# A decoder layer on one core: first weights and x as contiguous blocks, pooling differences issued sooner, centres before scales

## The chip, the cores and the metric

The kernel runs on one core of one Trainium2 chip. The metric is the device time of one execution in microseconds. The kernel before took 388.74 us (median of three runs, 388.48 to 389.14).

## What is computed

One layer of a decoder for 256 tokens of width 1024, in float32. The input x is projected once (w_in): 512 columns u for a pooling mixer and 512 each of q, k and v for attention with 8 heads of 64. With 256 tokens and blocks of 256 there is one block, so that the attention is plain causal softmax. The pooling mixer takes trailing-window means minus the token, for four windows of 128 channels each, then a linear map for each group:

```python
for g, w in enumerate((2, 4, 8, 16)):
    groups.append((c_hi - c_lo) / count - uf[..., sl])     # sums over the last w tokens
mixed = jnp.einsum('bsgc,gcd->bsgd', pooled, w_pool)
mix = concat([mixed * pool_scale, attention], -1) @ w_out
h = layer_norm(2**0.25 * x + mix, ln1_g, ln1_b)
h = layer_norm(2**0.25 * h + cross_attention(h, mem, w_xq, w_xkv, w_xo), ln2_g, ln2_b)
h = layer_norm(2**0.25 * h + (silu(h @ w_gate) * (h @ w_up)) @ w_down, ln3_g, ln3_b)
```

The cross-attention has 4 heads of 256 over 256 memory tokens; the feed-forward width is 2816.

## The kernel before, in words

**Products.** Each float32 operand is split into a high part of type float32r (a cast on ScalarE, `nc.scalar.copy`, L92 for weights and L300 for activations) and a low part, the rest (a subtraction on VectorE, L93 and L301). A product is three matmuls that add up in a PSUM bank: high x high, high x low, low x high (`three`, L234, and the like in `proj_t` and `product_qk`).

**The stream of weights.** `Stream` (L42) holds all weight tiles w0 to w124 in the order of their use. `fetch` issues the DMA of a tile into a raw buffer (seven of them; the first seven tiles have homes of their own), nearly always on the SyncE queue (SP). `prepare` makes the high and the low part of the next tiles and then fetches further ones; a raw buffer is free again when VectorE has made the low part. `get` hands out a tile and prepares up to eight tiles ahead. The order of the instructions on each engine is the order in which the Python program issues them; nothing is reordered, so that what stands behind a waiting instruction on its engine waits too.

**The start (L358 to L381).** `keep_busy(9)` fills TensorE with matmuls of zeros (`spark`, made by a VectorE memset) while the first data come. Then x^T arrives in pieces `xr` (tile rows 0, 1, 2-3, 4-5, 6-7) and the weights of q and k, columns 512 to 1535 of w_in, in tile rows of 128 x 1024, the first three in two halves of 512 columns each (w0 to w5). w0 goes through the queue of ScalarE, all others through SP. `product_qk(k)` (L341) multiplies tile row k into four banks: for each half of 512 columns the matmuls with the high part of the weights, each column block with xTh and then xTl, then those with the low part. Then follow v (w11 to w14), u (w15 to w18) and the keys of the memory, `xk` (w19 to w26).

In DRAM, w_in is an array of 1024 rows of 8 KB, and x_t one of 128 rows of 8 KB. A transfer of w0 reads 128 pieces of 2 KB, 8 KB apart; one of x's first tile rows 128 pieces of 1 KB, 8 KB apart; v's tiles have 2 pieces of 2 KB for each partition.

**Attention and pooling, interleaved by hand (L502 to L541).** `run(gen, n)` advances a projection by n steps, each of three matmuls for xk and u. Between the steps stand the pieces of attention (`scores`, `probs_t`, `attend`) and of the pooling: when half of u is done, ScalarE copies it to `upad` (L490) and GpSimd adds up the windows (`windows`, L457); VectorE subtracts (`pool_diff`, L467: upad = win / w - upad, in place), TensorE multiplies by w_pool (`mix_pool`, bank `pm`, L473), ScalarE and VectorE split the result. `probs_t` (banks `pt`, L433 to L435) transposes probabilities, and VectorE copies them to `sb` (L438). Banks of this kind rotate through four PSUM buffers.

**Norms (`Norm`, L548).** `sum` adds residual and product (L562), `measure` takes statistics (L565), `stats` joins them (L570, L572) and lets GpSimd raise the variance to the power -0.5 (L573, `rs`). `centre` is (r - mean) * g (L578, needs no `rs`), `scale` is r * rs + b (L584). `finish` (L587) does centre and scale for the first 512 columns, then for the others. Behind the second norm, `transpose_tok` (bank `tp`, L311) turns the result for the next product: the transposes of the first 128 tokens are placed between the last steps of the xo projection (L730 to L735), those of the second 128 between steps of the first gate product `gu0` (L757 to L762).

**The tail (L782 to L824).** The down projection of the second 128 tokens ends in pieces of 512, 256 and 256 columns. The sums of the first 512, of the next 256 and of the last 256 columns stay in their PSUM banks (`in_bank`, L806, and L820), and `finish` (L786) centres and scales them in the order centre 0-511, centre 512-767, scale 0-511, store, scale 512-767, store (on ScalarE's queue), centre 768-1023, scale 768-1023, store.

Of the kernel before, what the change touches and what calls it, by code (L numbers as in the profile page):

```python
# [8 lines left out]
F32 = mybir.dt.float32  # L9
# [5 lines left out]
P = 128  # L15
D = 1024
S = 256
T = S // P
KD = D // P
# [18 lines left out]
def r32(t):  # L38
    return t.bitcast(F32)


class Stream:  # L42


    def __init__(self, nc, pool):
        self.nc, self.pool = nc, pool
        self.src, self.raws, self.tiles, self.homes = [], [], [], []
        self.loads, self.splits = {}, {}
        self.used, self.held = 0, True
        self.pace, self.asked = 1, 0  # L50

    def add(self, src, parts=2):

        n = src.shape[1] // parts
        first = len(self.src)
        self.src += [src[:, i * n:(i + 1) * n, :] for i in range(parts)]
        return range(first, len(self.src))
# [9 lines left out]
    def fetch(self, upto, queue):  # L67

        while len(self.raws) < min(upto, len(self.src)):
            i = len(self.raws)  # L70
            for load in self.loads.pop(i, []):
                load()
            src = self.src[i]
            if i < len(self.homes):
                raw = self.homes[i]
            else:
                raw = self.pool.tile(list(src.shape), F32, tag="raw", name=f"w{i}r", bufs=RAW_BUFS)
            queue.dma_start(raw, src)
            self.raws.append(raw)

    def prepare(self, upto, eng=None):
        nc = self.nc
        while len(self.tiles) < min(upto, len(self.src)):
            i = len(self.tiles)
            src = self.src[i]
            for split in self.splits.pop(i, []):
                split()
            self.fetch(i + 1, nc.sync)
            raw = self.raws[i]
            hi = self.pool.tile(list(src.shape), F32R, tag="hi", name=f"w{i}h")  # L90
            lo = self.pool.tile(list(src.shape), F32R, tag="lo", name=f"w{i}l")
            nc.scalar.copy(hi, raw)  # L92
            (eng or nc.vector).tensor_sub(lo, raw, r32(hi))  # L93
            self.tiles.append((hi, lo))
            self.fetch(max(i + 1, len(self.homes)) + RAW_BUFS, nc.sync)
# [21 lines left out]

@with_exitstack
def decoder_layer(
    ctx: ExitStack, tc: tile.TileContext, x, x_t, mem_t, w_in, w_u, w_pool, pool_scale, w_out,  # L120
    ln1_g, ln1_b, w_xq, w_xk, w_xkv, w_xo, ln2_g, ln2_b, w_gu, w_down, ln3_g, ln3_b, out,
):
    nc = tc.nc
# [20 lines left out]
    ws = Stream(nc, wp)  # L144

    def cols(w, c):

        return ws.add(w[c])

    def rows(w, k0, c0, nk=1, width=D):  # L150
        return ws.add(w[k0 * P:(k0 + nk) * P, c0:c0 + width].rearrange("(k p) n -> p k n", p=P), 1)

    c_qk = [ws.add(w_in[k * P:(k + 1) * P, 512:1536].rearrange("p (j n) -> p j n", j=2), 2 if k < 3 else 1)
            for k in range(KD)]
    c_v = [rows(w_in, k, 1536, 2, 512) for k in range(0, KD, 2)]
# [11 lines left out]
    xT = (a8("xTh", F32R), a8("xTl", F32R))  # L167
# [5 lines left out]
    xr = a8("xr")  # L173
# [2 lines left out]
    ws.homes += [home[1][:, 0:1, :], home[1][:, 1:2, :], home[1][:, 2:4, :]]  # L176

    def load_xt(k, n=2):
        nc.sync.dma_start(xr[:, k:k + n, :], x_t[:, k:k + n, :])

    def split_xt(k, n=2):
        split(xT[0][:, k:k + n, :], xT[1][:, k:k + n, :], xr[:, k:k + n, :])
# [7 lines left out]
    def split_mem(k):  # L190
        split(mT[0][:, k:k + 4, :], mT[1][:, k:k + 4, :], mr[0][:, k:k + 4, :])
# [49 lines left out]
    def pair(hl, *ix):  # L241
        return hl[0][ix], hl[1][ix]
# [48 lines left out]
    def run(gen, n=None):  # L291

        while n is None or n > 0:
            if next(gen, gen) is gen:
                return False
            n = None if n is None else n - 1
        return True

    def split(h, l, ps):
        nc.scalar.copy(h, ps)  # L300
        nc.vector.tensor_sub(l, ps, r32(h))  # L301
# [17 lines left out]
    def keep_busy(n):  # L319

        ps = bank("busy")
        spark = ep.tile([P, P], F32, name="spark")
        nc.vector.memset(spark, 0.0)  # L323
        for _ in range(n):
            nc.tensor.matmul(ps[:, :P], spark, spark, start=True, stop=True)  # L325

# [14 lines left out]
    def product_qk(k):  # L341

        x_hi, x_lo = pair(xT, ALL, k)
        for j in range(2):
            hi, lo = ws.get(c_qk[k], j)
            for part in (((hi, x_hi), (hi, x_lo)), ((lo, x_hi),)):
                for i in (2 * j, 2 * j + 1):
                    for f in range(2):
                        c = 2 * (i % 2) + f
                        for n, (w, y) in enumerate(part):  # L350
                            nc.tensor.matmul(qk[i][:, f, :], w[:, c * P:(c + 1) * P], y,  # L351
                                             start=k == 0 and f == 0 and n == 0 and w is hi,
                                             stop=k == KD - 1 and w is lo, skip_group_check=True)
                    if k == KD - 1 and w is lo:
                        keep_qk(i)
            ws.done(c_qk[k], j)
# [14 lines left out]
    for g, w in enumerate(WINDOWS):  # L371
        nc.vector.tensor_scalar(fac[:, g, :], cnt, float(w), 1.0 / w, op0=OP.min, op1=OP.mult)
    nc.vector.reciprocal(fac, fac)
    split_xt(0, 1)
    ws.prepare(2)
    split_xt(1, 1)
    ws.held = False
# [89 lines left out]
    def pool_diff(g):  # L467
        pl = upad[:, g, PADW:]
        nc.vector.scalar_tensor_tensor(pl, sums[g][:, PADW:], 1.0 / WINDOWS[g], pl, op0=OP.mult, op1=OP.subtract)
# [32 lines left out]
    v, u, xk = do_v(), do_u(), do_xk()  # L502
# [27 lines left out]
    mix_pool(1)  # L530
# [17 lines left out]
    class Norm:  # L548
# [78 lines left out]
    for t in range(T):  # L627
        norm = Norm(1, xt[:, t, :], h1[:, t, :])
# [79 lines left out]
    xo = project(c_xo, lambda k: (oT[0][:, k], oT[1][:, k]), 4)  # L708
# [13 lines left out]
    norm = Norm(2, h1[:, 0, :], h2[:, 0, :])  # L722
# [33 lines left out]
    first = [accbank("pg") for t in range(T)]  # L756
# [47 lines left out]
    finish(norm, 0, (None, None, None))  # L804
# [22 lines left out]
_INS = ["x", "x_t", "mem_t", "w_in", "w_u", "w_pool", "pool_scale", "w_out", "ln1_g", "ln1_b", "w_xq", "w_xk",  # L827
        "w_xkv", "w_xo", "ln2_g", "ln2_b", "w_gu", "w_down", "ln3_g", "ln3_b"]


# [32 lines left out]
```

## Time and profile before

| | |
|---|---|
| three runs | 388.48, 388.74, 389.14 us |
| the profiled execution, its time | 388.8 us |
| its span in the profile | 387.0 us |
| granted clock of TensorE | 0.994 |
| moved by DMA | 71.91 MB, mean 186 GB/s |
| share of the span in the chain that ended last: PE, DVE, DMA, ACT | 88%, 5%, 2%, 2% |

Times in the profile are microseconds from the start of the span. PE is TensorE, PEld its weight loads, DVE VectorE, ACT ScalarE, POOL GpSimd, SP SyncE. A row of the timeline gives start, duration, engine, line, operation, what is written from what, shapes, how many instructions the row merges, and in brackets how long the engine idled before and what ended that. A row of the list of waits gives who waited for whom, the total in us, how often, and the longest. A row of the table of windows gives the window, its length, each engine's busy time with its count of instructions, then the granted clock, the busy share of the 16 DMA engines and GB/s. Durations of matmuls are modelled and overlap; the distance from start to start is their pace.

### The profile page before, as it was taken

To read this page: it belongs to the slowest core of one execution; us is meant where nothing else is said; L and a number is where in the kernel's file an instruction comes from. 1 tells how busy PE (TensorE), PEld (TensorE's weight loads), DVE (VectorE), ACT (ScalarE), POOL (GpSimd) and SP (SyncE) were. 2 spreads that over 40 slices of the span, in tenths; PEclk is the share of its full clock that TensorE was granted. 3 is DMA by queue.
4 is the path that set the end of the run, shared out by engine and by line. 5 is a ranking of instruction groups with operands and counts; after the bars stand their busy time and mean duration, and the time that the engine had idled before them with its cause. 6 is when DMAs were issued, how large, how long until landed. Compare 5 with 4: busy or idle time off the path is not lost.

```text
span 387.0 us, 5476 instructions
## 1 busy us (share of the span) xinstructions
PE 377.0 (97%) x2120; PEld 327.5 (85%) x2120; DVE 251.5 (65%) x362; ACT 179.8 (46%) x262; POOL 19.3 (5%) x31
## 2 busy tenths in 40 slices
PE   8999999999999999999999999999999999999992
PEld 8997988998888899988878888888888888888882
DVE  4777889855589767665889655556565555444176
ACT  4756676643253744545147553545554454343000
POOL 1000035300020000000100000000000000000000
PEclk9999999999999999999999999999999999999997
DMA  7998684458607963443108956565557655630011
GB/s 205 405 405 304 205 290 167 169 174 290 191 1 227 408 232 113 132 140 109 56 0 295 358 168 210 166 205 176 186 195 265 223 164 169 213 108 2 0 41 68
DMA packets 21689, 71.91 MB, mean 186 GB/s; under 512 B 2464, under 2 KB 3232, under 8 KB 21536
## 3 DMA queue, kind: packets, MB, share of 16 engines
q1 hardware_dynamic: 21232, 71.05, 53.3%
q10 hardware_dynamic: 432, 0.52, 0.4%
q8 instruction: 16, 0.26, 0.3%
q14 instruction: 9, 0.07, 0.0%
HBM read 70.52 MB, written 1.05 MB: 185 GB/s over the span
## 4 chain that ended last, share of the span: by engine, by line
PE 88%; DVE 5%; DMA 2%; ACT 2%; issue 1%; SPq 1%; POOL 0%; DVEq 0%; POOLq 0%; ACTq 0%
PE pg L239 10%; PE pg L237 10%; PE pg L238 10%; PE acc L237 8%; PE acc L239 8%; PE acc L238 8%; PE pxq L255 6%; PE pxk L255 5%; PE pqk L351 5%; DMA wr<-in_w_in 2%; PE xv L239 2%; PE xv L237 2%; PE xv L238 2%; PE pu L255 1%; PE pgt L751 1%; PE pv L237 1%
## 5 line engine op out<-in xcount | busy, mean ns | idle before, releaser
L573 POOL TENSOR_TENSOR rs<-rs,mhalf 128x1 f32<-128x1 f32 x6 | 5.4, 892 | 305.4 <-DVE rs L572 305.4
L744 ACT ACTIVATE sg<-pg 128x256 f32<-128x256 f32 x22 | 8.4, 384 | 12.9 <-PE pg L239 12.8
L562 DVE SCALAR_TENSOR_TENSOR r<-h,acc 128x256 f32<-128x256 f32 (+1 forms) x9 | 4.8, 532 | 10.9 <-PE acc L239 10.9
L745 DVE TENSOR_TENSOR sg<-sg,pg 128x256 f32<-128x256 f32 x22 | 9.2, 420 | 4.0 <-ACT sg L744 2.6
L387 ACT ACTIVATE pr<-pr,mx 128x128 f32<-128x128 f32 (+1 forms) x16 | 7.1, 445 | 6.7 <-DVE mx L418 6.7
L300 ACT CAST h2Th<-tp 128x512 fp32r<-128x512 f32 x4 | 2.4, 588 | 13.7 <-PE tp L311 13.7
L300 ACT CAST gTh<-pgt 128x512 fp32r<-128x512 f32 x11 | 6.0, 589 | 5.8 <-PE pgt L751 5.8
L387 ACT ACTIVATE xpr<-xs,mx 128x256 f32<-128x256 f32 x8 | 3.7, 469 | 10.2 <-DVE mx L398 10.2
L301 DVE TENSOR_TENSOR gTl<-pgt,gTh 128x512 fp32r<-128x512 f32 x11 | 7.1, 686 | 2.0 <-ACT gTh L300 1.5
L578 DVE SCALAR_TENSOR_TENSOR r<-r,mv,g 128x512 f32<-128x512 f32 (+1 forms) x11 | 7.6, 695 | 0.0
L565 DVE BATCH_NORM_STATS2 st<-r 128x6 f32<-128x512 f32 (+1 forms) x12 | 7.3, 605 | 0.4
L584 DVE SCALAR_TENSOR_TENSOR h<-r,rs,b 128x512 f32<-128x512 f32 x8 | 6.0, 752 | 1.9 <-POOL rs L573 1.8
L462 POOL TENSOR_TENSOR win<-upad 128x271 f32<-128x271 f32 x4 | 4.0, 988 | 55.6 <-ACT upad L490 55.6
L462 POOL TENSOR_TENSOR win<-win 128x269 f32<-128x269 f32 (+2 forms) x6 | 6.0, 993 | 0.5
L392 DVE RECIPROCAL sm<-sm 128x2 f32<-128x2 f32 x12 | 2.0, 166 | 5.9 <-ACT xpr L387 4.5
L751 PEld LDWEIGHTS pgt<-ident,sg 128*128 128x128 f32 x44 | 5.2, 140 | 0.8
L751 PE MATMUL pgt<-ident,sg 128*128 128x128 f32 x44 | 5.8, 272 | 0.0
L311 PEld LDWEIGHTS tp<-ident,h 128*128 128x128 f32 x32 | 3.8, 141 | 2.0 <-issue 0.7
L300 ACT CAST h1Th<-tp 128x512 fp32r<-128x512 f32 x4 | 2.3, 587 | 6.5 <-PE tp L311 6.5
L311 PE MATMUL tp<-ident,h 128*128 128x128 f32 x32 | 4.8, 274 | 0.4 <-DVE h L584 0.3
L325 PE MATMUL busy<-spark 128*128 128x128 f32 x18 | 4.2, 430 | 1.1 <-DVE spark L323 1.1
L305 DVE SCALAR_TENSOR_TENSOR xq<-pxq,xq 128x512 fp32r<-128x512 f32 x4 | 2.8, 691 | 3.3 <-ACT xq L304 3.3
(1092 smaller groups left out, 1424.8 us busy)
## 6 DMA issues: line engine op xcount, KB each, us to landing
g<-in_ln_g SPq DMA_DIRECT2D x3, 512.0 KB, 5.8
b<-in_ln_b SPq DMA_DIRECT2D x3, 512.0 KB, 6.7
wr<-in_w_in SPq DMA_DIRECT2D x5, 256.0 KB, 6.0
mr<-in_mem_t SPq DMA_DIRECT2D x1, 1024.0 KB, 11.1
xt<-in_x SPq DMA_DIRECT2D x1, 1024.0 KB, 8.0
xr<-in_x_t SPq DMA_DIRECT2D x3, 256.0 KB, 8.1
wr<-in_w_in SPq DMA_DIRECT2D x1, 512.0 KB, 8.1
w7r<-in_w_in SPq DMA_DIRECT2D x1, 512.0 KB, 8.1
```

Source lines behind the costliest of these rows:

```text
L237: nc.tensor.matmul(ps, wa, ya, start=start, stop=False, skip_group_check=part)
L238: nc.tensor.matmul(ps, wa, yb, start=False, stop=False, skip_group_check=part)
L239: nc.tensor.matmul(ps, wb, ya, start=False, stop=stop, skip_group_check=part)
L255: nc.tensor.matmul(pss[f], w[:, s], y, start=k == 0 and f == 0 and n == 0, stop=k == KD - 1 and n == 2, skip_group_check=True)
L300: nc.scalar.copy(h, ps)
L311: nc.tensor.transpose(ps[:, k * P:(k + 1) * P], tok[:, (k0 + k) * P:(k0 + k + 1) * P], ident)
L351: nc.tensor.matmul(qk[i][:, f, :], w[:, c * P:(c + 1) * P], y, start=k == 0 and f == 0 and n == 0 and w is hi, stop=k == KD - 1 and w is l ...
L387: nc.scalar.activation(dst[:, j, :], src[:, j, :], AF.Exp, bias=mx[:, j:j + 1], scale=sign, accum_out=sm[:, j:j + 1])
L462: nc.gpsimd.tensor_add(nxt[:, 2 * n - 1:], cur[:, 2 * n - 1:], cur[:, n - 1:PADW + S - n])
L744: nc.scalar.activation(sg, ps[:, :CW], AF.Silu, bias=0.0, scale=1.0)
L745: nc.vector.tensor_mul(sg, sg, ps[:, CW:])
L751: nc.tensor.transpose(pt[:, f, t * P:(t + 1) * P], sgs[c][:, t, f * P:(f + 1) * P], ident)
```

## The change

1. **DRAM layout.** The host lays the columns of q, k and v out as `w_qkv`, one contiguous block for each transfer, in the order [partition][row group][column]; x_t likewise (blocks of tile rows 0, 1, 2-3, 4-5, 6-7). Sizes and order of the transfers stay, and so do the shapes in SBUF.
2. **First tile in halves.** w0 is loaded by two transfers of 256 columns, both on ScalarE's queue, and cast in two parts. The product with tile row 0 takes all matmuls with xTh first, then those with xTl. The first xTh is made by VectorE, not by ScalarE.
3. **Zeros.** The busy loop reads a constant 0.0 that the program sets up at its start, instead of a tile that VectorE clears.
4. **Pooling.** `pool_diff(0)` and `pool_diff(1)` are issued behind `split_mem(4)`, ahead of the rest of u, and so ahead of the splits of w23 to w26 on VectorE.
5. **Norms.** `finish` centres both halves, then scales both. In the second norm three steps of xo, not two, are run ahead of the sum and the first transposes.
6. **Tail.** `finish` centres 0-511 and 512-1023, then scales 0-511, 512-767, 768-1023 with a store behind each. For the second 128 tokens the sums of columns 512 to 1023 go to SBUF (`norm.r`) instead of staying in PSUM.

```diff
@@ Stream
+        self.cuts = {}
...
-            queue.dma_start(raw, src)
+            for s in self.parts(i):
+                queue.dma_start(raw[:, :, s], src[:, :, s])
...
+    def parts(self, i):
+
+        return self.cuts.get(i, [slice(0, self.src[i].shape[2])])
...
-            nc.scalar.copy(hi, raw)
+            for s in self.parts(i):
+                nc.scalar.copy(hi[:, :, s], raw[:, :, s])
@@ decoder_layer
-    c_qk = [ws.add(w_in[k * P:(k + 1) * P, 512:1536].rearrange("p (j n) -> p j n", j=2), 2 if k < 3 else 1)
-            for k in range(KD)]
-    c_v = [rows(w_in, k, 1536, 2, 512) for k in range(0, KD, 2)]
+    def block(w, at, shape):
+
+        j, n = shape
+        return w[at:at + P * j * n].rearrange("(p j n) -> p j n", p=P, j=j)
+
+    c_qk = []
+    for k in range(KD):
+        if k < 3:
+            first = [ws.add(block(w_qkv, (2 * k + j) * P * 512, (1, 512)), 1)[0] for j in range(2)]
+            c_qk.append(range(first[0], first[1] + 1))
+        else:
+            c_qk.append(ws.add(block(w_qkv, k * P * 1024, (2, 512)), 1))
+    c_v = [ws.add(block(w_qkv, (KD + i) * P * 1024, (2, 512)), 1) for i in range(KD // 2)]
+    ws.cuts[0] = [slice(0, 256), slice(256, 512)]
...
-        nc.sync.dma_start(xr[:, k:k + n, :], x_t[:, k:k + n, :])
+        nc.sync.dma_start(xr[:, k:k + n, :], block(x_t, k * P * S, (n, S)))
...
-        spark = ep.tile([P, P], F32, name="spark")
-        nc.vector.memset(spark, 0.0)
+        spark = nc.const_aps.tensor(0.0, [P, P], F32)
...
-            for part in (((hi, x_hi), (hi, x_lo)), ((lo, x_hi),)):
+            parts = (((hi, x_hi),), ((hi, x_lo),)) if k == 0 else (((hi, x_hi), (hi, x_lo)),)
+            for part in (*parts, ((lo, x_hi),)):
...
-    split_xt(0, 1)
+    nc.vector.tensor_copy(xT[0][:, 0, :], xr[:, 0, :])
+    nc.vector.tensor_sub(xT[1][:, 0, :], xr[:, 0, :], r32(xT[0][:, 0, :]))
...
     split_mem(4)
+    pool_diff(0)
+    pool_diff(1)
     run(u)
-    run(xk, 6)
-    pool_diff(0)
-    run(xk, 6)
+    run(xk, 12)
     probs_t(2)
     mix_pool(0)
-    pool_diff(1)
     run(xk, 8)
@@ Norm.finish
             for half in HALVES:
                 self.centre(*half)
+            for half in HALVES:
                 self.scale(*half)
...
-    run(xo, 2)
+    run(xo, 3)
     norm.sum(*HALVES[0], acc0)
     transpose_tok(h2T, h2[:, 0, :], 0, 0)
@@ finish, tail
-    def finish(norm, t, at):
+    def finish(norm, t, at=None):

         norm.stats()
-        norm.centre(0, 512, at[0])
-        norm.centre(512, 768, at[1])
-        norm.scale(0, 512, at[0])
+        norm.centre(0, 512, at)
+        norm.centre(512, D)
+        norm.scale(0, 512, at)
         store(t, norm.r, 0, 512)
-        norm.scale(512, 768, at[1])
+        norm.scale(512, 768)
         store(t, norm.r, 512, 768, nc.scalar)
-        norm.centre(768, D, at[2])
-        norm.scale(768, D, at[2])
+        norm.scale(768, D)
         store(t, norm.r, 768, D)
...
-    in_bank(norm, right[:, :256], 512, 768)
+    norm.add(512, 768, right[:, :256])
     last = until(dn)[1]
-    nc.vector.tensor_add(last, norm.r[:, 768:], last)
-    nc.vector.bn_stats(norm.st[:, norm.n, :], last)
-    norm.n += 1
-    finish(norm, 1, (left, right[:, :256], last))
+    nc.vector.tensor_add(norm.r[:, 768:], norm.r[:, 768:], last)
+    norm.measure(768, D)
+    finish(norm, 1, left)
```

More of the change, by code (lines that the diff above doesn't have):

```diff
@@ L119, in decoder_layer @@
 def decoder_layer(
-    ctx: ExitStack, tc: tile.TileContext, x, x_t, mem_t, w_in, w_u, w_pool, pool_scale, w_out,
+    ctx: ExitStack, tc: tile.TileContext, x, x_t, mem_t, w_qkv, w_u, w_pool, pool_scale, w_out,
     ln1_g, ln1_b, w_xq, w_xk, w_xkv, w_xo, ln2_g, ln2_b, w_gu, w_down, ln3_g, ln3_b, out,
@@ L351, in product_qk @@
                             nc.tensor.matmul(qk[i][:, f, :], w[:, c * P:(c + 1) * P], y,
-                                             start=k == 0 and f == 0 and n == 0 and w is hi,
+                                             start=k == 0 and f == 0 and w is hi and y is x_hi,
                                              stop=k == KD - 1 and w is lo, skip_group_check=True)
@@ L803, in decoder_layer @@
             norm.add(half[0] + c, half[0] + c + 256, acc[:, c:c + 256])
-    finish(norm, 0, (None, None, None))
+    finish(norm, 0)
     def in_bank(norm, acc, c0, c1):
@@ L817, in decoder_layer @@
     norm.sum(768, D, right[:, 256:])
-    in_bank(norm, right[:, :256], 512, 768)
+    norm.add(512, 768, right[:, :256])
     last = until(dn)[1]
-    nc.vector.tensor_add(last, norm.r[:, 768:], last)
-    nc.vector.bn_stats(norm.st[:, norm.n, :], last)
-    norm.n += 1
-    finish(norm, 1, (left, right[:, :256], last))
+    nc.vector.tensor_add(norm.r[:, 768:], norm.r[:, 768:], last)
+    norm.measure(768, D)
+    finish(norm, 1, left)
     run(dn)
-_INS = ["x", "x_t", "mem_t", "w_in", "w_u", "w_pool", "pool_scale", "w_out", "ln1_g", "ln1_b", "w_xq", "w_xk",
+_INS = ["x", "x_t", "mem_t", "w_qkv", "w_u", "w_pool", "pool_scale", "w_out", "ln1_g", "ln1_b", "w_xq", "w_xk",
         "w_xkv", "w_xo", "ln2_g", "ln2_b", "w_gu", "w_down", "ln3_g", "ln3_b"]
@@ L849, with blocks @@
     given["pool_scale"] = given["pool_scale"].reshape(4, P).T
-    given["x_t"], given["mem_t"] = transposed(given["x"]), transposed(given["mem"])
+    def blocks(a, groups):
+        a = a.reshape(-1, P, a.shape[1])
+        return np.concatenate([a[g].transpose(1, 0, 2).ravel() for g in groups])
+    w_in, pairs = given["w_in"], [[k, k + 1] for k in range(0, KD, 2)]
+    given["x_t"] = blocks(given["x"].T, [[0], [1]] + pairs[1:])
+    given["mem_t"] = transposed(given["mem"])
+    first = w_in[:3 * P, 512:1536].reshape(3, P, 2, 512).transpose(0, 2, 1, 3)
+    given["w_qkv"] = np.concatenate([first.ravel(), w_in[3 * P:, 512:1536].ravel(), blocks(w_in[:, 1536:], pairs)])
     given["w_u"], given["w_xk"] = chunks(given["w_in"][:, :512]), chunks(given["w_xkv"][:, :D])
```

## The prediction

> **What bounds the kernel now.** I read the shares of busy time first, then the list of what TensorE waited for, then the timeline around each wait in it.
>
> ```profile
> PE 377.0 (97%) x2120; PEld 327.5 (85%) x2120; DVE 251.5 (65%) x362; ACT 179.8 (46%) x262; POOL 19.3 (5%) x31
> ```
>
> ```profile
> PE busy L325 <- DVE spark L323: 1.1, 1, 1.1
> PE pm L473 <- DVE upad L469: 0.9, 1, 0.9
> PE tp L311 <- DVE h L584: 0.3, 1, 0.3
> PE pqk L351 <- ACT w4h L92: 0.2, 1, 0.2
> ```
>
> TensorE is busy for 377.0 us of a span of 387.0, and the second list is complete: in the whole kernel its matmuls waited four times, 2.5 us in all. The matmuls themselves are not changed (same shapes, same count). So only three places can give time back: the start, the two waits in the middle (pm, tp), and the tail behind the last matmul. The profiled execution took 388.8 us, of which 1.8 lie outside the span; the median of the runs is 388.74, 0.06 lower, so the sum below can be set against either. A measurement of this kernel can tell about 0.2%, 0.8 us, from no change.
>
> **A. The start (block layout, halves, constant spark, xTh on VectorE).**
>
> ```profile
> 0.83 0.17 DVE L323 MEMSET spark<- 128x128 f32 x1 [0.83 <-PEq L836]
> 1.05 4.21 PE L325 MATMUL busy<-spark 128*128 128x128 f32 x18 [1.05 <-DVE spark L323]
> 4.05 0.61 ACT L92 CAST w0h<-wr 128x512 fp32r<-128x512 f32 x1
> 4.92 0.56 PE L351 MATMUL pqk<-xTh,w0h 128*128 128x256 f32 x1
> ...
> 6.34 0.41 PE L351 MATMUL pqk<-xTh,w0h 128*128 128x256 f32 x1
> 6.55 0.32 PE L351 MATMUL pqk<-xTl,w0h 128*128 128x256 f32 x1
> ...
> 8.64 0.39 PE L351 MATMUL pqk<-xTh,w2h 128*128 128x256 f32 x1
> ...
> 11.14 0.64 PE L351 MATMUL pqk<-xTh,w3l 128*128 128x256 f32 x4
> 11.30 0.62 ACT L92 CAST w4h<-wr 128x512 fp32r<-128x512 f32 x1 [0.95 <-DMA wr<-in_w_in]
> 11.97 0.38 PE L351 MATMUL pqk<-xTh,w4h 128*128 128x256 f32 x1 [0.19 <-ACT w4h L92]
> ```
>
> The zero matmuls of the busy loop (L325) start 0.2 us after the memset that they wait for may start. Reading a constant that lies there already, they start at about 0.85 and end about 0.2 earlier. The first real matmul follows them at 4.92, while w0h was ready at 4.05 + 0.61 = 4.66: the busy loop, not the data, sets it. Hence 4.70 after, and the halves of w0 and the copy of xTh on VectorE (off ScalarE) matter only in that they must not be late: first half of w0h, 256 columns, about 4.4. Until 6.55 matmuls come every 0.21 us (6.34 to 6.55), then the 20 from 8.64 to 11.14 every 0.125. With the faster pace beginning at the same instant, 1.85 / 0.21 = 8.8 of the 24 matmuls of the first row of tiles are slow, 15.2 take 0.12, and the row ends at 8.4, not at 8.64 (w2 must be there by then, too). That alone buys nothing, because of w4: its cast begins when the transfer lands (11.30), and TensorE, done with w3l at 11.14 + 4 x 0.12 = 11.62, stands until 11.97. So the start is worth something only if the loads land sooner. Do they?
>
> ```profile
> 2.00:4.00 2.00, 2.00 (x12) 2.00 (x11) 0.96 (x5) 0.72 (x2) 0.15 (x3) 1.00 1.01 310
> 4.00:7.00 3.00, 3.00 (x17) 3.00 (x17) 1.81 (x3) 1.28 (x3) 0.00 (x0) 1.00 0.85 117
> 7.00:10.00 3.00, 3.00 (x26) 2.94 (x26) 1.80 (x3) 1.93 (x4) 0.00 (x0) 1.00 1.04 377
> ```
>
> The last column is GB/s, the one before it the busy share of the DMA engines. From 4 to 7 us the engines are 0.85 busy yet move 117 GB/s, a third of what they move before and after. 3 us at 117 instead of 377 is 0.78 MB not moved, 2.1 us at 377. What is in flight then, by the order of the issues on SP, are the second row of x (1 KB pieces, 8 KB apart in DRAM) and w2 (2 KB pieces, 8 KB apart). Busy engines with few bytes mean that single pieces take long, which is what a scattered read could do and a contiguous block need not. w4 must land 0.6 us earlier than 11.30 to be ready when TensorE asks; that is under a third of the 2.1 us. Bounds of A: 0 if the slow stretch stays; 0.25 + 0.35 = 0.6 if it shrinks by a third or more; up to 0.4 on top if the pace also changes 0.9 us sooner. I take **0.6**, since a third is little of what is there to win.
>
> By the Trainium skill (DMA: Bandwidth & Descriptors, Latency and other measured facts) a large power-of-two row pitch slows copies, but its table begins at a 512 KiB pitch and there loses almost nothing; so at 8 KB the layout should not matter. The 377 GB/s after 7 us, with the same 8 KB pitch, agree with it, the 117 ahead of them do not; rival 1 is that case.
>
> **B. The pooling differences ahead of w23 to w26 on VectorE.**
>
> ```profile
> 56.91 0.22 POOL L464 TENSOR_TENSOR win<-win,fac 128x16 f32<-128x16 f32 x1
> ...
> 59.20 1.22 DVE L301 TENSOR_TENSOR mTl<-mr,mTh 128x1024 fp32r<-128x1024 f32 x1
> ...
> 63.94 0.27 PE L435 MATMUL pt<-ident,pr 128*128 128x128 f32 x1
> 64.20 0.85 DVE L469 SCALAR_TENSOR_TENSOR upad<-win,upad 128x256 f32<-128x256 f32 x1
> 64.97 1.65 DVE L93 TENSOR_TENSOR w26l<-w26r,w26h 128x1024 fp32r<-128x1024 f32 x1
> 65.10 0.70 PE L473 MATMUL pm<-upad,wpl 128*128 128x256 f32 x2 [0.89 <-DVE upad L469]
> 66.54 0.68 DVE L438 COPY sb<-pt 128x512 f32<-128x512 f32 x1
> 68.72 0.27 PE L435 MATMUL pt<-ident,pr 128*128 128x128 f32 x1
> 70.97 0.42 DVE L469 SCALAR_TENSOR_TENSOR upad<-win,upad 128x256 f32<-128x256 f32 x1
> ```
>
> pm for group 0 waits for upad, which stands in VectorE's queue behind three splits. In the new order two differences follow mTl directly, at 60.34; GpSimd has the windows of groups 0 and 1 by 56.91 + 0.22 = 57.13, so the new wait ends before it begins. They take 0.42 each beside an idle GpSimd (0.85 beside a busy one) and are done by 61.2, or 62.0 at worst, over 2 us before pm. TensorE leaves pt at 63.94 + 0.11 and starts pm at about 64.15: **0.95 us** gained, between 0.9 (the wait itself) and 1.05. Behind the moved instructions the splits of w23 to w25 come 0.8 later, and with them the SP loads that reuse their raw buffers; w23 is first multiplied after the 12 last matmuls of w20 and 24 each of w21 and w22, 60 x 0.12 = 7 us behind pm, which hides it. What is late next is sb: upad of group 1, formerly behind it, now precedes it, so it starts about 0.4 later, 66.95 to 67.63. Its bank is rewritten by the third transpose of the next pt, at 68.72, which moves to 67.75. That is 0.1 us of cover; if the splits run long beside GpSimd, up to 0.4 comes back here.
>
> **C. The tail.**
>
> ```profile
> 380.90 0.75 DVE L578 SCALAR_TENSOR_TENSOR acc<-acc,mv,g 128x512 f32<-128x512 f32 x1
> 381.13 0.55 POOL L573 TENSOR_TENSOR rs<-rs,mhalf 128x1 f32<-128x1 f32 x1 [6.70 <-DVE rs L572]
> 381.56 0.48 DVE L578 SCALAR_TENSOR_TENSOR acc<-acc,mv,g 128x256 f32<-128x256 f32 x1
> 381.95 0.74 DVE L584 SCALAR_TENSOR_TENSOR r<-acc,rs,b 128x512 f32<-128x512 f32 x1
> ...
> 383.52 0.48 DVE L584 SCALAR_TENSOR_TENSOR r<-acc,rs,b 128x256 f32<-128x256 f32 x1
> ```
>
> Up to 381.56 the chain keeps its length (one add, one statistics, the same small ones). Then: a centre of 512 instead of 256 (0.67 instead of 0.39), a scale of 512 (0.66), a scale of 256 (0.39), a scale of 256 (0.48 to its end): 381.56 + 0.67 + 0.66 + 0.39 + 0.48 = 383.76, against 383.52 + 0.48 = 384.00. The last store and what follows it move with it: 0.24 gained. The new centre has both inputs in SBUF and meets GpSimd's power, which lasts until 381.68; if one holds the other up, 0.12 to 0.3 of it goes. I take **0.2**, from -0.1 to 0.3.
>
> By the Trainium skill (SBUF — State Buffer, Who interferes with whom) whichever of the two starts first holds the shared port for its whole instruction; the power starts first here, so the centre would wait 0.12 and C be 0.12. The power's 0.55 beside a PSUM operand fits, but no row here has that order of the two.
>
> **D. Norms: both centres, then both scales; the first transpose one step later (three steps of xo, not two).**
>
> ```profile
> 188.52 0.74 DVE L578 SCALAR_TENSOR_TENSOR r<-r,mv,g 128x512 f32<-128x512 f32 x1
> 189.70 0.75 DVE L584 SCALAR_TENSOR_TENSOR h<-r,rs,b 128x512 f32<-128x512 f32 x1 [0.44 <-POOL rs L573]
> ...
> 191.15 0.75 DVE L584 SCALAR_TENSOR_TENSOR h<-r,rs,b 128x512 f32<-128x512 f32 x1
> 191.28 0.59 ACT L300 CAST h2Th<-tp 128x512 fp32r<-128x512 f32 x1 [6.94 <-PE tp L311]
> ...
> 192.42 0.68 DVE L301 TENSOR_TENSOR h2Tl<-tp,h2Th 128x512 fp32r<-128x512 f32 x1
> ...
> 198.17 0.63 PE L311 MATMUL tp<-ident,h 128*128 128x128 f32 x4 [0.31 <-DVE h L584]
> ...
> 199.10 0.40 PE L239 MATMUL pg<-w62h,h2Tl 128*128 128x512 f32 x1
> 199.62 0.63 PE L311 MATMUL tp<-ident,h 128*128 128x128 f32 x4
> ```
>
> VectorE idles 0.44 us for GpSimd's power between centre and scale. With the second centre in that hole (it follows 0.67 behind the first, as 381.56 behind 380.90 above) the first scale starts at 188.52 + 2 x 0.67 = 189.86, 0.16 later, and the second at 190.53, 0.62 earlier. TensorE reads the first half first. In the second token block the same order costs the first tp 0.16, and the moved transpose some 0.18: it comes three matmuls, 3 x 0.23 = 0.69 us, later, and its split on VectorE stood 192.42 - 191.28 - 0.59 = 0.55 behind its data. So tp at 198.17 becomes 198.5. From there TensorE needs 199.10 + 0.23 - 198.17 = 1.16 us to the second tp, which no longer waits for its scale: 199.66 instead of 199.62. D costs **0.05**, with 0.15 either way. In the first norm TensorE has the xv product between result and transposes, and no wait of it stands in the list, so nothing there counts.
>
> **Sum:** 0.6 + 0.95 + 0.2 - 0.05 = 1.7; 388.8 - 1.7 = **387.1** (387.04 from the median).
>
> **Rivals.**
> 1. The loads land when they did: the slow stretch belongs to the start of the stream, not to the layout (the first pieces of x and w, just as scattered, ran at 310 GB/s). Then w4 still ends the wait at 11.97, A is 0: 388.8 - 1.1 = **387.7**. Chance 0.28.
> 2. B's wait comes back as one for sb or for a split run long beside GpSimd: half of 0.95 is lost, **387.5**. Chance 0.08.
> 3. Slower: the slow stretch moves forward onto the first tile. Its first weights now come as 1 KB pieces, the size that x's second row had in the slow stretch. At 117 GB/s the first tile lands up to 3 us later than now; TensorE runs dry behind the busy loop and starts at 7.7 instead of 4.92. 2.8 later, less the 0.5 of waits at 8.64 and 11.97 that it absorbs, less B, C and D (1.1): 388.8 + 1.2 = **390.0**. It decides from a first matmul at 6.5 on (4.92 + 0.5 + 1.1). Against it: that size ran fast from 2 to 4 us. Chance 0.06.
>
> **How the numbers follow.** The forecast has 0.52; 0.06 is for what I don't see. Low end: A 1.0, B 1.05, C 0.3, D 0.1 gained, 2.45 in all, 386.3. High end: rival 1 with half of B lost and C at 0.1, 0.5 in all: 388.3. The bound of 0.2% lies at 387.96. Forecast, most of rival 1 and rival 2 lie below: faster 0.82. What remains of rival 1 and both together: same 0.12. Rival 3: slower 0.06.
>
> **What would show it.** First real matmul at 4.7, and the wait for w4h gone, with over 250 GB/s from 4 to 7 us (A; if that window stays near 117, rival 1). No pm row in TensorE's waits, upad done before 62 (B; a pt or attend wait on sb is rival 2). 4.2 us from the last add to the end of the last scale instead of 4.4 (C). The first tp 0.3 later than A and B alone would put it, the second where they put it (D). A first matmul behind 6.5 is rival 3.

## The result and the profile after

The changed kernel takes 386.31 us in the median (386.20 to 386.89, six runs) against 388.91 (388.48 to 389.24, six runs): a ratio of 0.9938, 95% interval 0.9925 to 0.9950. A second set of five runs of it gave 386.35, ratio 0.9945 (0.9933 to 0.9958). By the first ratio it is faster by 2.4 us (1.9 to 2.9), where 1.7 was forecast. The profiled execution took 386.2 us with a span of 384.4; the span before was 387.0, so the trace has 2.60 us to explain. It is the fastest execution of its six; the median lies 0.1 higher, the slowest 0.7.

The list of TensorE's waits, complete (who waited for whom, total us, times, longest):

```profile
PE busy L342 <- PEq L853: 0.8, 1, 0.8
PE pqk L369 <- ACT w0h L99: 0.5, 1, 0.5
PE tp L329 <- DVE h L602: 0.4, 1, 0.4
```

The rows of pm and of w4h are gone. New is a wait for w0h: the second half of the first tile. The start in the timeline of the kernel after:

```profile
0.77 3.58 PE L342 MATMUL busy<-const-float32-0.0 128*128 128x128 f32 x18 [0.77 <-PEq L853]
...
4.11 0.48 PE L369 MATMUL pqk<-xTh,w0h 128*128 128x256 f32 x2
4.62 0.40 ACT L99 CAST w0h<-wr 128x256 fp32r<-128x256 f32 x1 [0.79 <-DMA wr<-in_w_qkv]
...
5.07 0.50 PE L369 MATMUL pqk<-xTh,w0h 128*128 128x256 f32 x2 [0.48 <-ACT w0h L99]
5.41 0.64 PE L369 MATMUL pqk<-xTl,w0h 128*128 128x256 f32 x4
...
7.97 0.62 ACT L99 CAST w4h<-wr 128x512 fp32r<-128x512 f32 x1
...
10.70 0.28 PE L369 MATMUL pqk<-xTh,w4h 128*128 128x256 f32 x1
```

Three things are to be seen. w4 is cast at 7.97 instead of 11.30, and TensorE takes it at 10.70 without a wait, 1.27 us earlier than 11.97. The busy loop starts at 0.77 (about 0.85 was forecast), and its 18 passes take 3.34 us to 4.11 (before: 1.05 to 4.92, 3.87). And the matmuls behind it come every 0.12 us at once (5.41 x4 to 5.89): the change of pace, at 6.55 before, lies inside the busy loop here. If a slow pass takes 3.87 / 18 = 0.215 and a fast one half of that, 13 of the 18 were slow, so that it changed at about 3.6. The row of the window from 4 to 7 us (last columns: granted clock, busy share of the DMA engines, GB/s):

```profile
4.00:7.00 3.00, 2.52 (x22) 2.32 (x21) 1.91 (x4) 2.16 (x5) 0.00 (x0) 1.00 1.04 355
```

355 GB/s stand where 117 stood. The granted clock reads 1.00 in both kernels in every window from 2 to 10 us, at the slow pace too: the pace is to be read from start to start.

The pooling, in the timeline of the kernel after:

```profile
58.97 0.76 DVE L488 SCALAR_TENSOR_TENSOR upad<-win,upad 128x256 f32<-128x256 f32 x2
...
62.56 0.27 PE L454 MATMUL pt<-ident,pr 128*128 128x128 f32 x1
62.67 0.60 PE L492 MATMUL pm<-upad,wpl 128*128 128x256 f32 x2
62.92 0.47 PE L273 MATMUL pxk<-mTh,w20h 128*128 128x256 f32 x1
...
65.51 0.68 DVE L457 COPY sb<-pt 128x512 f32<-128x512 f32 x1
```

In the timeline of the kernel before, the first product behind pm:

```profile
65.45 0.47 PE L255 MATMUL pxk<-mTh,w20h 128*128 128x256 f32 x1
```

Both differences are done by 59.73, and pm follows pt by 0.11 us. The last pt before pm came 1.38 earlier than before (63.94 to 62.56), the first product behind it (w20h) 2.53 earlier (65.45 to 62.92): A gave 1.38, B 1.15.

The second norm, timeline of the kernel after:

```profile
195.80 0.63 PE L329 MATMUL tp<-ident,h 128*128 128x128 f32 x4 [0.40 <-DVE h L602]
...
196.95 0.60 PE L329 MATMUL tp<-ident,h 128*128 128x128 f32 x4
```

The first tp is 2.37 earlier than before (198.17), so 0.16 of the 2.53 is lost; the second is 2.67 earlier (199.62), so it is more than made up. Further on the distance settles at 2.60.

The tail, first the last add in the timeline of the kernel before, then the timeline of the kernel after, whose span ends at 384.4:

```profile
379.60 0.43 DVE L820 TENSOR_TENSOR acc<-r,acc 128x256 f32<-128x256 f32 x1
```

```profile
377.00 0.42 DVE L838 TENSOR_TENSOR r<-r,acc 128x256 f32<-128x256 f32 x1 [0.62 <-PE acc L257]
...
378.28 0.75 DVE L596 SCALAR_TENSOR_TENSOR acc<-acc,mv,g 128x512 f32<-128x512 f32 x1
378.51 0.55 POOL L591 TENSOR_TENSOR rs<-rs,mhalf 128x1 f32<-128x1 f32 x1 [6.69 <-DVE rs L590]
378.94 0.74 DVE L596 SCALAR_TENSOR_TENSOR r<-r,mv,g 128x512 f32<-128x512 f32 x1
379.60 0.75 DVE L602 SCALAR_TENSOR_TENSOR r<-acc,rs,b 128x512 f32<-128x512 f32 x1
380.26 0.87 DVE L602 SCALAR_TENSOR_TENSOR r<-r,rs,b 128x256 f32<-128x256 f32 x2
```

From the last add to the end of the last scale it is 377.00 to 381.13, 4.13 us instead of 4.40 (379.60 to 384.00): the 0.27 is there. But the span ends 3.27 behind the last scale, not 3.00 (387.0 - 384.00). From the last add to the end it is 7.40 in both kernels. So the sum of the trace: A 1.38, B 1.15, D 0.07, C 0 = 2.60.

### The profile page after: what moved, and what is told of

Read it like the earlier page. It is cut to its first block, busy times and chain, and to the rows that moved or that the text cites. A ratio compares the mean times of both kernels' runs of the same rounds, so it can differ in the third digit from the quotient of the medians.

```text
span 384.4 us, 5475 instructions
## 1 busy us (share of the span) xinstructions
PE 375.3 (98%) x2120; PEld 326.2 (85%) x2120; DVE 250.0 (65%) x360; ACT 179.2 (47%) x262; POOL 19.3 (5%) x31
## 3 DMA queue, kind: packets, MB, share of 16 engines
HBM read 70.52 MB, written 1.05 MB: 186 GB/s over the span
## 4 chain that ended last, share of the span: by engine, by line
PE 95%; DVE 2%; DMA 1%; issue 0%; ACT 0%; ACTq 0%; DVEq 0%
PE pg L257 10%; PE pg L256 10%; PE pg L255 10%; PE acc L255 9%; PE acc L257 9%; PE acc L256 9%; PE pqk L369 6%; PE pxq L273 6%; PE pxk L273 6%; PE pu L273 3%; PE xv L257 2%; PE xv L255 2%; PE xv L256 2%; PE pgt L770 1%; PE pv L255 1%; PE pv L256 1%
## 5 line engine op out<-in xcount | busy, mean ns | idle before, releaser
L583 DVE BATCH_NORM_STATS2 st<-r 128x6 f32<-128x512 f32 (+1 forms) x14 | 8.1, 579 | 0.4
L596 DVE SCALAR_TENSOR_TENSOR r<-r,mv,g 128x512 f32<-128x512 f32 x11 | 7.8, 743 | 0.0
L437 DVE CUSTOM_DVE_ANT_0 pr<-ps,tri 128x128 f32<-128x128 f32 (+1 forms) x16 | 4.7, 352 | 0.2 <-PE ps L430 0.2
```

## The experiments

Each ran beside the kernel before, and each ratio is against those executions of it. One table ahead of the reasons: time of the median, ratio with its interval, and from each profiled execution its own time, the GB/s from 4 to 7 us, and when TensorE began the third and the fifth tile (w2h, w4h).

| kernel | median us | ratio (95%) | profiled us | GB/s 4-7 | w2h at | w4h at |
|---|---|---|---|---|---|---|
| before | 388.74 | | 388.8 | 117 | 8.64 | 11.97 |
| after | 386.31 | 0.9938 (0.9925-0.9950) | 386.2 | 355 | 7.81 | 10.70 |
| e1 before, block layout | 387.69 | 0.9974 (0.9965-0.9982) | 388.31 | 295 | 8.70 | 11.58 |
| e2 after, old layout | 387.81 | 0.9978 (0.9968-0.9989) | 387.85 | 179 | 8.63 | 12.13 |
| e12 after, x_t in old layout | 386.59 | 0.9949 (0.9935-0.9962) | 386.79 | 304 | 8.35 | 11.23 |
| e4 before, constant zeros | 388.62 | 0.9995 (0.9986-1.0004) | 389.0 | 152 | 8.52 | 12.17 |
| e8 after, memset zeros | 386.84 | 0.9955 (0.9943-0.9967) | 387.41 | 340 | 8.89 | 11.77 |
| e7 after, w0 in one piece | 386.12 | 0.9935 (0.9921-0.9949) | 386.78 | 346 | 8.44 | 11.31 |
| e10 after, again | 386.35 | 0.9945 (0.9933-0.9958) | 386.33 | 315 | 7.93 | 10.81 |
| e3 before, pooling moved | 387.46 | 0.9969 (0.9956-0.9981) | 387.22 | 149 | 8.31 | 11.54 |
| e6 before, norms | 388.67 | 1.0001 (0.9993-1.0010) | 388.65 | 142 | 8.47 | 11.82 |
| e5 before, tail | 388.81 | 1.0005 (0.9996-1.0013) | 388.82 | 154 | 8.37 | 11.96 |
| e9 e7 with four stores | 386.35 | 0.9938 (0.9925-0.9950) | 386.87 | 318 | 8.60 | 11.48 |
| e11 after, one store less | 386.46 | 0.9938 (0.9925-0.9952) | 386.58 | 335 | 8.50 | 11.38 |

### Is it the layout? (e1, e2, e12)

e1 is the kernel before with the blocks in DRAM and nothing else (q, k, v and x_t; two of the lines):

```diff
-    c_qk = [ws.add(w_in[k * P:(k + 1) * P, 512:1536].rearrange("p (j n) -> p j n", j=2), 2 if k < 3 else 1)
...
+            c_qk.append(ws.add(block(w_qkv, k * P * 1024, (2, 512)), 1))
...
-        nc.sync.dma_start(xr[:, k:k + n, :], x_t[:, k:k + n, :])
+        nc.sync.dma_start(xr[:, k:k + n, :], block(x_t, k * P * S, (n, S)))
```

> The kernel before with the block layout of w_in's columns and of x_t alone (one transfer for w0, memset zeros, old order). Theory L (the layout removes the slow stretch): over 250 GB/s from 4 to 7 us, no wait for w4h, and the scores of the first block start 0.6 to 1.1 us sooner; median 0.6 to 1.1 below the kernel before. Rival S (the slow stretch belongs to the start of the stream and only vanished because transfers were issued otherwise): near 117 GB/s from 4 to 7 us, the wait for w4h stays, time as before within 0.2. Pace of the matmuls: if its change hangs on when TensorE gets busy (1.05 here as before), it stays near 6.5; if on the data's arrival, it moves.

e2 is the reverse: the changed kernel with these lines as before.

> The changed kernel with the old DRAM layout, all else kept (halves, constant zeros, xTh on VectorE, pooling, norms, tail). Theory L: near 117 GB/s from 4 to 7 us again, a wait for w4h or w2h, and A shrinks to 0.3 or less: 387.3 to 387.7. Rival S: over 250 GB/s stays and the time is that of the changed kernel, 386.3, within 0.2.

Of e1, the row of the window:

```profile
4.00:7.00 3.00, 3.00 (x16) 3.00 (x16) 1.98 (x4) 1.70 (x4) 0.00 (x0) 1.00 0.89 295
```

Of e2, the same window and the row of TensorE's waits for w4h:

```profile
4.00:7.00 3.00, 2.56 (x16) 2.27 (x16) 1.29 (x3) 1.33 (x3) 0.00 (x0) 1.00 0.85 179
```

```profile
PE pqk L359 <- ACT w4h L99: 0.5, 1, 0.5
```

The layout alone lifts 117 to 295 GB/s, takes the wait for w4h away (11.58 in the table, without one) and gains 0.7 to 1.4 us. e1's trace shows only half of this: its scores start 0.49 sooner (30.34 instead of 30.83), not 0.6 to 1.1. Its profiled execution, 388.31, is the slowest of its eleven, and its pace changes late, at about 6.8; no trace shows the faster ones. Taken out of the changed kernel, the slow stretch and the wait are back, and 1.5 us are lost (387.81 to 386.31; 387.3 to 387.7 was expected). All five kernels on the old layout with changes elsewhere moved 142 to 179 GB/s in that window; all on blocks moved 295 or more. Theory L holds; rival S falls.

Which pieces? e12 puts only x_t back:

```diff
-        nc.sync.dma_start(xr[:, k:k + n, :], block(x_t, k * P * S, (n, S)))
+        nc.sync.dma_start(xr[:, k:k + n, :], x_t[:, k:k + n, :])
```

> The changed kernel with x_t alone back in its old layout (1 KB and 2 KB pieces 8 KB apart); the weights stay in blocks. If it is the 1 KB pieces of x that are slow (theory X): 120 to 200 GB/s from 4 to 7 us, a wait for w4h or w2h, and a time like that of the old layout, 387.3 to 387.9. If it is the weights' rows (theory W): over 300 GB/s, no such wait, 386.3 within 0.3. If both share it: 200 to 300 GB/s and 386.4 to 387.2.

```profile
4.00:7.00 3.00, 2.98 (x18) 2.69 (x18) 2.02 (x5) 2.09 (x5) 0.00 (x0) 1.00 1.03 304
```

The window of e12 stays at 304 GB/s with x in rows, and w2h and w4h are not waited for; the median is 0.24 to 0.28 above that of the changed kernel. All three are just inside what was expected of theory W. But windows of 1 us show a slow stretch in e12 too, only later:

```profile
6.00:7.00 1.00, 1.00 (x10) 1.00 (x10) 1.00 (x4) 0.80 (x2) 0.00 (x0) 1.00 0.96 178
7.00:8.00 1.00, 1.00 (x11) 1.00 (x10) 0.89 (x3) 0.62 (x1) 0.00 (x0) 1.00 0.79 205
```

The changed kernel moved 340 and 369 GB/s in these two, and none of the seven kernels with all in blocks less than 285. e12's cast of w4 begins at 9.61, against 7.97 to 9.18 in those seven and 10.87 to 11.50 in the six with all in rows. So the rows of x alone bring a slow stretch as well. It costs no wait, because w4h is ready at 10.23 and used at 11.23. Theory W in its pure form falls with this: the window from 4 to 7 us was the wrong one to tell the theories apart. Whether the rows of the weights alone would be slow was not run. Why rows are slow for two or three us and fast before and after stays open; the blocks also lie elsewhere in DRAM, which was not tried apart.

### What sets the pace? (e4, e8, e10)

e4 is the kernel before with the constant zeros alone, e8 the changed kernel without them:

```diff
-        spark = ep.tile([P, P], F32, name="spark")
-        nc.vector.memset(spark, 0.0)
+        spark = nc.const_aps.tensor(0.0, [P, P], F32)
```

> The kernel before with the constant zeros alone. Theory P (the earlier start of the busy loop moves the change of pace from 6.55 to about 3.6): the busy loop ends by 4.2, the first real matmul waits for w0h until 4.7, and TensorE then stands for w4h as before, so the time gains 0 to 0.2 at most. Rival Q (the change of pace is not tied to the start of the busy loop): the loop ends 0.2 to 0.3 earlier at about 4.65, the pace changes elsewhere; the time is as before within 0.2 as well. The place of the change tells them apart, not the time.

> The changed kernel with the zeros made by VectorE's memset again, so that the busy loop starts at about 1.05. Theory P: the pace changes near 6.5 again, the busy loop ends at 4.9, and the first row of tiles takes 0.8 to 0.9 longer; time 386.9 to 387.2. Rival Q: the pace changes at about 3.6 as in the changed kernel, and the time is 386.3 to 386.5, since the second half of w0h (4.62 + 0.40) sets the start of the row anyhow.

e4's TensorE waits:

```profile
PE pqk L350 <- ACT w4h L92: 0.5, 1, 0.5
PE pqk L350 <- ACT w2h L92: 0.5, 1, 0.5
```

On the old layout an earlier start of TensorE turns into longer waits for w2h and w4h, and nothing is gained. e4's first real matmul comes at 4.89 and not by 4.7, and the matmuls behind it come every 0.12 from 5.11 on, so the change of pace lies ahead of 4.89. In e8 the first row of tiles runs slowly to its end:

```profile
4.91 1.20 PE L370 MATMUL pqk<-xTh,w0h 128*128 128x256 f32 x4
5.91 1.05 PE L370 MATMUL pqk<-xTl,w0h 128*128 128x256 f32 x4
```

Four matmuls take 0.85 to 1.0 from group to group (the next starts at 6.76), 0.48 at the fast pace. e8 loses 0.5 against the changed kernel. By itself that fits theory P (the start of the busy loop moves the change of pace). So the changed kernel was run once more, and the same start stands in e11:

> The changed kernel once more, unchanged. If the place of the change of pace is chance (theory Q), it need not lie at 3.6 again; by the profiles so far anywhere from 3.6 to 6.7, and the first row of tiles ends between 7.8 and 8.9 accordingly. If it belongs to the kernel, it lies at 3.6 within 0.2. Median 386.3 within 0.2.

Rows of e10's timeline, then of e11's:

```profile
4.61 1.10 PE L369 MATMUL pqk<-xTh,w0h 128*128 128x256 f32 x4
5.55 0.63 PE L369 MATMUL pqk<-xTl,w0h 128*128 128x256 f32 x4
```

```profile
4.61 1.20 PE L369 MATMUL pqk<-xTh,w0h 128*128 128x256 f32 x4
5.61 1.05 PE L369 MATMUL pqk<-xTl,w0h 128*128 128x256 f32 x4
```

The same instructions, the same start at 0.77 or 0.78, and the pace changes at about 3.6 in the first profile, between 4.61 and 5.55 in e10, behind 6.4 in e11. With the start at 1.05 the place varies as well: 6.55 in the kernel before, about 5.2 in e5 (every 0.12 from 5.27 on), ahead of 5.0 in e6. P falls: the start does not set the place of the change, which differs between executions by some 3 us. What hangs on it is w2h at 7.81, 7.93 or 8.50, 0.7 us. Of the 0.5 that e8 loses, 0.28 can be the later start (1.05 instead of 0.77); how much of the rest is chance its five runs can't tell.

### Do the halves of w0 help? (e7)

```diff
-    ws.cuts[0] = [slice(0, 256), slice(256, 512)]
```

> The changed kernel with w0 in one piece (one transfer, one cast), all else kept. Theory H0 (the halves gain nothing, because the second half lands when the whole would): w0h ready at 4.3 to 4.6 in one, TensorE starts with one wait and passes through the first row without the 0.48 in its middle; time 386.3 within 0.2, or 0.1 to 0.3 lower, as one transfer is issued sooner than two. Rival H1 (the first half bridges to the second): the first matmul is 0.4 to 0.5 later and the row ends as much later, 386.7 or more.

```profile
4.65 1.22 PE L368 MATMUL pqk<-xTh,w0h 128*128 128x256 f32 x4
```

e7 has no wait for w0h, and a late change of pace (four matmuls in 1.02 from 4.65 on). 386.12 against 386.31 and 386.35: the intervals overlap, so the halves gain nothing that shows (H0). The order of the matmuls with xTh and xTl and the copy of xTh on VectorE were not run alone.

### Pooling and norms alone (e3, e6)

e3 moves `pool_diff(0)` and `pool_diff(1)` behind `split_mem(4)` in the kernel before, as the diff of the change has it:

> The kernel before with the pooling differences moved alone. Theory B (the whole wait of pm goes and nothing is late next): no pm row among TensorE's waits, upad done before 62, the time 0.95 to 1.15 below the kernel before, about 387.65. Rival (half comes back as a wait for sb or a later split): a pt or attend row in the waits and 0.5 below, about 388.2.

Its waits of TensorE, complete:

```profile
PE busy L325 <- DVE spark L323: 1.1, 1, 1.1
PE tp L311 <- DVE h L583: 0.3, 1, 0.3
```

No pm, no pt, no attend: theory B, and 0.7 to 1.7 us in time. The row of w4h is missing too, although e3 has the old layout: w4 landed sooner in this execution (cast at 10.87, not 11.30), and w4h starts at 11.54; the 0.22 to the matmul behind it is the mark of a wait, which is too short for the list. So of the 1.6 us between the spans (385.4 and 387.0) only a part is the pooling's. The last pt comes at 63.49, 0.45 sooner, and w20h at 63.85, 1.60 sooner: 1.15 for the pooling, as in the changed kernel. e6 has the order of the norms and the third step of xo alone:

```diff
             for half in HALVES:
                 self.centre(*half)
+            for half in HALVES:
                 self.scale(*half)
...
-    run(xo, 2)
+    run(xo, 3)
     norm.sum(*HALVES[0], acc0)
```

> The kernel before with the norms' order and the third step of xo alone. As recorded: first tp some 0.16 to 0.3 later, the second tp without a wait, sum within 0.1 of the kernel before, 388.6 to 388.8. Rival: without the other parts the second tp is as late as the first, and 0.2 to 0.3 is lost, 389.0.

388.67 against 388.60: nothing, as recorded; the rival's 0.2 to 0.3 is not seen. In its trace the second tp has no wait.

### Where the tail's gain goes (e5, e11, e9)

e5 is the kernel before with the new `finish` and the sums of columns 512 to 1023 in SBUF.

> The kernel before with the new tail alone. Theory T0 (the end is set by the landing of the last three stores, which now follow one another so closely that their bytes queue): 4.1 us from last add to the end of the last scale, then 3.3 instead of 3.0 to the end of the span, 7.4 from last add to the end as before; time as before within 0.1. Rival T1 (the tail is worth its 0.27, and the other kernels' ends are chance): 3.0 behind the last scale, 7.1 in all, time 0.2 to 0.3 lower.

e5's timeline:

```profile
core 0 of [0], span 387.0 us
...
379.59 0.42 DVE L819 TENSOR_TENSOR r<-r,acc 128x256 f32<-128x256 f32 x1 [0.61 <-PE acc L239]
...
382.86 0.87 DVE L584 SCALAR_TENSOR_TENSOR r<-r,rs,b 128x256 f32<-128x256 f32 x2
```

The last scale ends at 383.73, 3.27 before the end; from the last add 7.41. The time is as before. The longer end is in every trace (spans are given to 0.1 us): 3.25 to 3.36 from the last scale to the end in seven kernels with the new tail, 2.92 to 3.00 in five with the old. Windows of the end, kernel before and then kernel after:

```profile
383.00:384.00 1.00, 0.00 (x0) 0.00 (x0) 0.96 (x3) 0.00 (x0) 0.00 (x0) 0.50 0.44 168
384.00:385.00 1.00, 0.00 (x0) 0.00 (x0) 0.01 (x1) 0.00 (x0) 0.00 (x0) 0.50 0.72 261
385.00:386.00 1.00, 0.00 (x0) 0.00 (x0) 0.00 (x0) 0.00 (x0) 0.00 (x0) 0.50 0.27 95
```

```profile
381.00:382.00 1.00, 0.00 (x0) 0.00 (x0) 0.13 (x1) 0.00 (x0) 0.00 (x0) 0.50 0.78 291
382.00:383.00 1.00, 0.00 (x0) 0.00 (x0) 0.00 (x0) 0.00 (x0) 0.00 (x0) 0.50 0.67 234
```

Before, the last store's bytes are a tail of their own; after, all 512 KB move together. e11 takes the first of the three stores away:

```diff
-        store(t, norm.r, 0, 512)
+        if t == 0:
+            store(t, norm.r, 0, 512)
```

> The changed kernel without the store of columns 0 to 511 of the second 128 tokens (these 256 KB of the output are left out, the arithmetic stays). T0 (the bytes queue): the end comes 2.8 to 3.0 after the last scale instead of 3.3, time 0.3 to 0.5 below the changed kernel. Rival (latency behind the last issue alone): 3.3 stays, time as the changed kernel.

```profile
core 0 of [0], span 384.8 us
...
377.69 0.42 DVE L839 TENSOR_TENSOR r<-r,acc 128x256 f32<-128x256 f32 x1 [0.61 <-PE acc L257]
...
380.96 0.87 DVE L602 SCALAR_TENSOR_TENSOR r<-r,rs,b 128x256 f32<-128x256 f32 x2
```

In e11's timeline the end comes 2.97 behind the last scale (384.8 - 381.83) and 7.11 behind the last add: the 0.27 appears as soon as the store ahead is gone. The five times do not show it: 386.46 misses the 0.3 to 0.5 that was expected. The pace alone can move a time by more (0.7 above). T0 holds by the trace: the first store delays the last. e9 tries to use it: w0 in one piece, and four scales of 256 columns with a store each, on two queues in turn.

```diff
-        norm.scale(0, 512, at)
-        store(t, norm.r, 0, 512)
...
+        for i, c in enumerate(range(0, D, 256)):
+            norm.scale(c, c + 256, at[:, c:c + 256] if at is not None and c < 512 else None)
+            store(t, norm.r, c, c + 256, nc.scalar if i % 2 else nc.sync)
```

> The changed kernel with w0 in one piece, and in the tail of both token blocks four scales of 256 columns with a store behind each, in turn on SP's and ScalarE's queue. If the end is set by the bytes of the stores that queue (T0), the first bytes start 0.27 earlier and the last piece is no larger: 0.1 to 0.25 less from the last add to the end, 7.15 to 7.3 instead of 7.4, and the time 0.1 to 0.3 below that of w0 in one piece (386.12). If each store has a fixed latency behind its issue, the extra scale costs its 0.1 and nothing is gained: 7.5.

```profile
core 0 of [0], span 385.1 us
...
377.79 0.42 DVE L834 TENSOR_TENSOR r<-r,acc 128x256 f32<-128x256 f32 x1 [0.49 <-PE acc L256]
...
381.18 0.87 DVE L601 SCALAR_TENSOR_TENSOR r<-r,rs,b 128x256 f32<-128x256 f32 x2
```

3.05 behind the last scale (385.1 - 382.05), but 7.31 from the last add: of the 0.2 saved behind the scale, 0.1 is paid for the fourth scale. The 0.1 that is left is no more than the traces differ: with the new tail and three stores it is 7.38 to 7.50. A miss: 386.35, not below 386.12. Whether the stores queue for the DMA engines or for the order of SP's queue was not tried apart. No kernel tried is measurably faster than the changed one.

## Why the prediction was right, and where not

**The sum.** 386.31 lies 0.01 above the low end of the range, 386.3, and that it lies inside is luck: in the trace A and B both go beyond the upper bounds from which that end was added up (1.0 and 1.05), and C's zero takes most of the excess back. The profiled execution itself, 386.2, is outside. The direction and the two large terms came from where they were forecast. Without the luck of one profile, by the ratios of the single changes: 1.0 for the layout (e1), 1.2 for the pooling (e3), and nothing clear of noise for e4, e5 and e6, together some 2.2 of the 2.4.

**A, 0.6 forecast, 1.38 in the trace, 1.0 for the layout alone by the times.** Right: w4 lands early enough, the wait for w4h goes, the slow stretch belongs to the layout (e1, e2), so rival 1 falls. The step that failed is "with the faster pace beginning at the same instant". 6.55 was one profile's value of something that varies from run to run between about 3.6 and 6.8. In e11, where the pace changes late too, w4h starts at 11.38, 0.59 sooner than before: the forecast 0.6. In the profiled execution after it changes about 3 us sooner, and w4h starts at 10.70, another 0.68; the text had allowed 0.4. On the old layout such luck was worth nothing, because the loads of w2 and w4 absorbed it (e4: two waits of 0.5; e5 and e6, whose pace changes early, have w4h at 11.96 and 11.82). So removing the wait also uncovered a variation that it had hidden. The last 0.1 of 1.38 is that the first matmul behind a wait costs more. In the timeline of the kernel before, the one behind the wait for w4h, at 11.97, is followed after 0.22, the next after 0.12:

```profile
12.19 0.28 PE L351 MATMUL pqk<-xTl,w4h 128*128 128x256 f32 x1
12.31 0.28 PE L351 MATMUL pqk<-xTh,w4h 128*128 128x256 f32 x1
```

That the pace differs from run to run is what the Trainium skill says (TensorE: Matmul & The Clock Gate, Part 1: The HAM clock gate (the "warmup" mystery)): the activity window that releases the clock runs freely, so that equal kernels see a different number of slow matmuls. The three profiles of one start agree with it, from 3.6 to behind 6.4 us; the granted clock of the windows, 1.00 at either pace, does not show it. The spread that the Trainium skill gives there, 0.5 us to either side, is smaller than the 3 us of these profiles; the measurement decides.

The prediction read the Trainium skill's table of row pitches (DMA: Bandwidth & Descriptors, Latency and other measured facts), which begins at 512 KiB, as saying that 8 KB should not matter. That reading goes beyond the table, and 117 to 179 GB/s with rows against 295 to 355 in blocks decide against it here.

**The halves** "matter only in that they must not be late". They were late by 0.48 in the profiled execution (second half cast at 4.62), because the busy loop ended at 4.11; where the pace changes late they are not (e10, e11: no such wait). In time the halves make no difference that shows (e7).

**B, 0.95 forecast, 1.15 in the trace.** pm starts 1.05 sooner relative to pt, the upper bound given: the list has 0.89 of it, because it counts from the modelled end of the matmul before. The matmul behind pm comes another 0.1 sooner, again what a wait costs beyond itself. e3 has the same 1.15. Nothing was late next: sb is copied at 65.51 and no wait on it is in the list, so rival 2 falls (e3).

**C, 0.2 forecast, 0 measured.** The 0.27 on VectorE came (4.13 us). Failed: "the last store and what follows it move with it". What follows lengthened from 3.00 to 3.27, for stores that come closer together delay one another (e5, e11). By the Trainium skill's rule of the shared port (SBUF — State Buffer, Who interferes with whom) the prediction had the centre wait 0.12 for GpSimd's power. No such wait shows: the centre at 378.94 follows the one at 378.28 by 0.66 and takes 0.66 to the next, beside the power's 0.55 from 378.51. As ends on GpSimd are rough in the profile, 0.12 us of overlap can't refute the rule.

**D, -0.05 forecast, +0.07 in the trace, nothing in time (e6).** The first tp is 0.16 later, the size forecast for the order of the centres; the 0.18 for the moved transpose did not come, and why was not tried. From the first tp to the second it is 1.15, as worked out (1.16).

**Rival 3** did not come: first matmul at 4.11 to 4.91 in all profiles with blocks.

## What to carry to other kernels

A wait that ends last hides what lies under it: before a term is priced at "the wait and no more", ask which quantity was absorbed by it, and whether the one profile at hand shows that quantity's usual value or one of many. Lay out the first transfers, on which everything waits, as contiguous blocks. Look for a slow stretch in windows shorter than it: an average over 3 us hid e12's. And at the end of a kernel, count from the last add to the end of the span, with the stores' bytes, not to the last instruction.

## What the runs showed of the hardware

- Rows of 2 KB (weights) and of 1 and 2 KB (x), 8 KB apart, moved 117 to 179 GB/s in the window from 4 to 7 us in six kernels with DMA engines 0.83 to 0.90 busy; the same tiles in blocks 295 to 355 in seven. Before 4 us and behind 7 us the kernel before moved 310 and 377. With x alone in rows the slow stretch came later, 178 and 205 GB/s from 6 to 8 us.
- TensorE's pace changed from 0.21 to 0.12 us a matmul at times between about 3.6 and 6.8 us, with one start of the busy loop; that was worth up to 0.7 us here, and the granted clock reads 1.00 on both sides.
- A matmul behind a wait took 0.22 instead of 0.12 to the next one: a removed wait, 0.9 in the list and 1.05 from start to start, gave 1.15.
- The end of the span came 2.97 us behind the last scale without the store of 256 KB ahead (e11), 3.25 to 3.36 with it (seven kernels).
